# Three quarters of a kernel's opening products from un-normed x, with g_pre folded into the weights

## The chip, the cores and the metric

The kernel runs on one core of a Trainium2 chip. The metric is the device time of one execution in microseconds. TensorE (PE) multiplies, VectorE (DVE) and ScalarE (ACT) work on tiles element by element, GpSimd (POOL) and SyncE (SP) mostly issue transfers here. Every engine takes its own instructions in order.

## The reference

One decoder layer, x of 512 tokens by 2048 channels, float32. What matters here is its first step:

```
h = x * rsqrt(mean(x * x, axis=-1) + 1e-6) * g_pre
[q | k | v | z_att | u | g_glu | z_conv] = h @ w_in
conv = layernorm(causal_conv31(u * sigmoid(g_glu)) + conv_b) ...
```

Attention over q, k, v, the convolution branch, an output projection and a second norm follow; they are computed as before.

## The kernel before

Every float32 factor is split into a rounded high part (hi) and a rest (lo), and a product is three matmuls: hi*hi, hi*lo, lo*hi. The high part is an ACT copy, the rest a DVE subtraction (`split`).

**The opening** computes the first 512 channels of g_glu, token rows by channels, in 16 blocks (kg, m): kg is one of four groups of 512 input channels, m one of four groups of 128 tokens. `turn_x` (`turn_block` in the plan) transposes the x tile of a block on PE in four 128x128 matmuls, ACT writes the high part `h_hi`, DVE the rest `h_lo`. `rows_block` is the block's 12 matmuls into the PSUM tile `gn` of its m; the transposes of the next block stand behind its first two matmuls. `part` splits a 128x512 piece of the weights (`r_gn` into `h_gn`, `l_gn`).

For kg = 0 the kernel already works without the norm: the weights are multiplied by g_pre (`g_col`), x is taken as it is, and each `gn` is later multiplied by its token's root (`scale_up`). For kg = 1 to 3 x is normed first: `square` and `root` give the root of each token, `broadcast_g` spreads g_pre over 128 partitions with two matmuls a group, and `scale_block` multiplies x by both before it is transposed. The normed h of kg = 0, which the later products need, is made by `norm_first` at the end of the opening from a kept copy of the transposed x (`whole`).

**The order.** PE's order is the order of the code. In the opening DVE and ACT too run in code order, given by the table `plan`: what stands behind each block's matmuls. Later DVE, ACT, SP and POOL are ordered by the scheduler.

**Behind the opening** come the first products of the pair u (`pair`): two steps of 48 matmuls, one for each half of the 2048 input channels, with weights `r_u` of 1 MB each. `turn_vectors` transposes the ten rows of conv_w, conv_b, ln_g, ln_b and b_pw2 into `vec` (tile `rows`, two halves of five transfers: 31 rows of 2 KB for conv_w, one row of 2 KB for each of the others). `turn_gates` transposes the finished g_glu (`g_nat`, copied from `gn`) into `gT`. Both stand inside the first step of u.

**Transfers.** SP's queue carries x, weights and `rows`. POOL's queue carries sums of weight blocks (`vs`, 1 MB each, some of them accumulating in DRAM), one issued after each block from the sixth on. A transfer from SP also waits until the one eight places before it has landed (the DMAHW numbers below go round from 0 to 7). Raw weights have two buffers, so a transfer into one waits until DVE has split what was there.

Of the kernel before, what the change touches and what calls it, by code (L numbers as in the profile page):

```python
# [16 lines left out]
P = 128  # L17
# [31 lines left out]
def hybrid_layer(  # L49
# [81 lines left out]
    pick = const.tile([4, 4, P], F32R, name="pick")  # L131
    for j in range(4):
        nc.gpsimd.tensor_copy(pick[:, j, :], ident[:4, j : j + 1].to_broadcast([4, P]))
# [15 lines left out]
    g_ks = early.tile([4, P], F32, name="g_ks")  # L149
    g_col = const.tile([P, 4], F32, name="g_col")  # L150
    g_rows = t2("g_rows")[:4]
    g_bc = {}

    def turn_g():

        ps = trp.tile([P, S], F32, tag="tr", name="g_col_ps")
        nc.tensor.transpose(ps[:, :4], g_ks, ident[:4, :4])
        nc.vector.tensor_copy(g_col, ps[:, :4])

    def split_g():  # L160
        g_parts = [t2(f"g_{part}", F32R)[:4] for part in ("hi", "lo")]
        split(*g_parts, g_rows)
        return g_parts

    def broadcast_g(j, g_hi, g_lo):

        ps = trp.tile([P, S], F32, tag="tr", name=f"g_ps{j}")
        nc.tensor.matmul(ps, pick[:, j, :], g_hi, start=True, stop=False)
        nc.tensor.matmul(ps, pick[:, j, :], g_lo, start=False, stop=True)
        g_bc[j] = t2(f"g_bc{j}")  # L170
        nc.vector.tensor_copy(g_bc[j], ps)
# [28 lines left out]

    def square(m, j, eng=None):
        junk = t2(f"junk{m}_{j}")
        total = sums[m][:, j : j + 1]
        if eng is None:
            nc.scalar.activation(junk, xts[m][j], AF.Square, accum_out=total)
        else:
            eng.tensor_tensor_reduce(
                out=junk, in0=xts[m][j], in1=xts[m][j], scale=1.0, scalar=0.0,
                op0=ALU.mult, op1=ALU.add, accum_out=total,
            )  # L210
# [3 lines left out]
    def root_table(m):  # L214
# [6 lines left out]
        rsqrt_table(y, v)  # L221
        roots[m] = y, v

# [15 lines left out]
    def turn_x(m, j):  # L239
# [9 lines left out]
        if j == 0:  # L249
            nc.scalar.copy(raw_h[m, 0], src)  # L250
        nc.vector.tensor_tensor(out=lo, in0=src, in1=f32(hi), op=ALU.subtract)

        def keep_raw():
            raw_h[m, j] = t2(f"xw{m}_{j}").rearrange("p (i t) -> p i t", i=4)
            nc.scalar.copy(raw_h[m, j], src)
# [21 lines left out]
    def norm_first():  # L277

        lo = {}
        for i in range(5):  # L280
            if i < 4:
                x, hi = whole[:, i, :], h_hi[0][:, i, :]
                nc.vector.scalar_tensor_tensor(
                    out=x, in0=x, scalar=g_col[:, i : i + 1], in1=rbc[0],
                    op0=ALU.mult, op1=ALU.mult,
                )
                nc.scalar.activation(hi, x, AF.Copy)
            if i > 0:
                nc.vector.tensor_tensor(
                    out=h_lo[0][:, i - 1, :], in0=whole[:, i - 1, :], in1=f32(h_hi[0][:, i - 1, :]),  # L290
                    op=ALU.subtract,
                )
            yield
# [39 lines left out]
    def pair(c0, post, name, halves=(0, 1)):  # L333
# [3 lines left out]
        def unit(half, i):  # L337
            def go(w):
                hi, lo = w
                if half == halves[0]:  # L340
                    ps[i] = mm(f"{name}_{i}")
                cs = slice(i * P, (i + 1) * P)
                for k in range(8):
                    mm3(
                        ps[i], (hi[:, k, cs], lo[:, k, cs]), h_at(half * 8 + k),
                        half == halves[0] and k == 0, half == halves[1] and k == 7,
                    )
                if half == halves[1]:
                    post(i, ps[i])
            return go  # L350

        for half in halves:
# [646 lines left out]
    def conv_in(t):  # L999
        if t > 1:  # L1000
            pair(C_G + t * 256, post_g(2 * t), f"g{t}")

        pair(C_U + t * 256, post_u(2 * t), f"u{t}", (0, 1) if t else (1, 0))
# [31 lines left out]
    with tc.manual_schedule(engines={mybir.EngineType.DVE, mybir.EngineType.Activation}):  # L1035
# [5 lines left out]
        def load_w0(kg, eng=nc.sync):  # L1041
            raw, hi, lo = (
                raws.tile([P, 4, S], F32, tag="raw", name=f"r_gn{kg}"),
                his.tile([P, 4, S], F32R, tag="hi", name=f"h_gn{kg}"),
                los.tile([P, 4, S], F32R, tag="lo", name=f"l_gn{kg}"),
            )
            w0[kg] = raw, hi, lo
            if kg == 0:
                for i in range(4):
                    eng.dma_start(raw[:, i], g_src(0)[i * P : (i + 1) * P, :])  # L1050
            else:
                eng.dma_start(raw, g_src(kg).rearrange("(k p) c -> p k c", p=P))

        def part(kg, i):
            raw, hi, lo = w0[kg]
            split(hi[:, i], lo[:, i], raw[:, i], g_col[:, i : i + 1] if kg == 0 else None)
# [11 lines left out]
        nc.sync.dma_start(g_ks, g_pre[: 4 * P].rearrange("(k p) -> k p", p=P))  # L1068
        load_x(0, 0)
        load_w0(0, nc.scalar)  # L1070
        nc.sync.dma_start(g_rows, g_pre.rearrange("(j c) -> j c", j=4))
        for m in range(1, NT):
            load_x(m, 0)
        load_x(0, 1, 2, 3)
        load_x(1, 1, 2, 3)
        load_w0(1)
        load_x(2, 1, 2, 3)
        load_x(3, 1, 2, 3)

        turn_g()  # L1080
        blocks = [(kg, m) for kg in range(4) for m in range(NT)]

# [10 lines left out]
        def do(f, *args):  # L1093
            return partial(f, *args)

        g_parts = []
        first = norm_first()
        keeps = {}

        plan = {  # L1100
            0: ([do(turn_block, 2)], [
                lambda: g_parts.extend(split_g()), do(square, 0, 1), do(square, 0, 2, dve),
                do(square, 0, 3),
            ]),
            1: ([do(turn_block, 3), lambda: broadcast_g(1, *g_parts)], [
                do(root_table, 0), do(square, 1, 1), do(square, 1, 2, dve), do(root, 0),
                do(square, 1, 3), do(root_table, 1), 
            ]),
            2: ([lambda: broadcast_g(2, *g_parts)], [
                do(scale_block, 4), do(part, 1, 0), do(scale_up, 0), do(root, 1),  # L1110
                do(scale_block, 5), do(part, 1, 1),
            ]),
            3: ([do(turn_block, 4), lambda: broadcast_g(3, *g_parts)], [
                do(square, 2, 1), do(part, 1, 2), do(square, 2, 2, dve), do(part, 1, 3),
                do(square, 2, 3), do(root_table, 2), do(scale_up, 1),
            ]),
            4: ([do(turn_block, 5)], [
                do(root, 2), do(scale_block, 6), do(square, 3, 1), do(square, 3, 2, dve),
                do(square, 3, 3), do(root_table, 3), do(scale_up, 2), do(load_w0, 2),
            ]),  # L1120
            5: ([do(turn_block, 6)], [
                do(root, 3), do(scale_block, 7), do(scale_up, 3), do(part, 2, 0), do(part, 2, 1),
            ]),
            6: ([do(turn_block, 7)], [do(scale_block, 8), do(part, 2, 2), do(part, 2, 3)]),
            7: ([do(turn_block, 8)], [do(scale_block, 9), do(scale_block, 10)]),
            8: ([do(turn_block, 9)], [do(load_w0, 3), do(scale_block, 11), do(part, 3, 0)]),
            9: ([do(turn_block, 10)], [do(scale_block, 12), do(part, 3, 1)]
                + [do(widen_root, m) for m in range(NT)]),
            10: ([do(turn_block, 11)], [
                load_vectors,  # L1130
                do(scale_block, 13), do(part, 3, 2), do(part, 3, 3)
            ]),
            11: ([do(turn_block, 12), broadcast_roots], [
                do(scale_block, 14)
            ]),
            12: ([do(turn_block, 13)], [
                do(scale_block, 15), lambda: loaded.update({0: steps[0].load()}),
            ]),
            13: ([do(turn_block, 14)], [do(keep_rows, 0)]),
            14: ([do(turn_block, 15)], [  # L1140
                do(keep_rows, 1), do(next, first)
            ]),
            15: ([], [do(next, first), do(keep_rows, 2), do(next, first)]),
        }
        loaded = {}
# [3 lines left out]
        turn_block(1)  # L1149
        for m in range(NT):  # L1150
            square(m, 0, dve)
        for n, (kg, m) in enumerate(blocks):
            if n < 4:
                for f in plan[n][0]:
                    f()
            rows_block(kg, m, ps0[m], w0[kg][1:], plan[n][0] if n >= 4 else ())
            for f in plan[n][1]:
                f()
            if 4 <= n + 1 < len(blocks):
# [4 lines left out]
        next(first)  # L1164
        next(first)
# [11 lines left out]

    heads_run = attention()
# [8 lines left out]
    for n, step in enumerate(steps):  # L1187
# [23 lines left out]
        if n + 1 < len(steps):  # L1211
# [43 lines left out]
```

## Time and profile before

| | |
|---|---|
| median of 3 runs | 878.05 us (875.48 to 878.66) |
| the profiled execution's own time | 875.07 us |
| its span in the profile | 873.4 us |
| PE busy | 852.9 us, 98% of the span |
| DVE, ACT, POOL busy | 625.2, 392.3, 125.9 us |

Busy is the time in which an engine had at least one instruction in work. The span is the profiled part of an execution; its own time is 1.7 us longer. A busy PE is not necessarily a PE at its full rate, since matmuls overlap: its rate is read from the starts of neighbouring matmuls.

### The profile page before, as it was taken

The page shows a single profiled execution, that of the slowest core. Times are in us where ns is not written, and L with a number is a line of the kernel's source. Part 1 is how long each engine was busy: PE and PEld are TensorE (multiplying, and loading weights), DVE is VectorE, ACT ScalarE, POOL GpSimd, SP SyncE. Part 2 cuts the span into 40 slices and gives each one's busy share as a digit, 9 for nine tenths or more (in the row PEclk, how much of TensorE's full clock was granted, in tenths as well). Part 3 has the DMA queues.
Part 4 walks back from the last instruction along what each step waited for, and adds up shares of the span by engine and source line. Part 5 has one row for each costly group of instructions (what it writes and reads, how often), then busy time and mean ns, then how long its engine had stood idle before and what let it go on. Part 6 is the DMA issues. An engine that isn't in the chain of part 4 may idle for free.

```text
span 873.4 us, 9762 instructions
## 1 busy us (share of the span) xinstructions
PE 852.9 (98%) x3879; PEld 706.5 (81%) x3879; DVE 625.2 (72%) x742; ACT 392.3 (45%) x447; POOL 125.9 (14%) x157
## 2 busy tenths in 40 slices
PE   6899999999999999999999999999999999999995
PEld 4688888888888888888888888888888888888884
DVE  5766889996697978969696984235643776458775
ACT  5653424645443543343322545235722346455542
POOL 0012110001202132213111233032001000000032
PEclk9999999999999999999999999999999999999998
DMA  9499994558587565875497547862232246556782
GB/s 300 160 266 257 282 278 149 193 192 293 192 191 150 176 204 130 174 188 185 144 189 151 190 147 191 167 171 96 90 104 97 97 158 227 193 193 259 283 275 98
DMA packets 87262, 163.32 MB, mean 187 GB/s; under 512 B 2978, under 2 KB 52134, under 8 KB 83440
## 3 DMA queue, kind: packets, MB, share of 16 engines
q1 hardware_dynamic: 70320, 111.31, 37.6%
q0 software_dynamic: 16320, 50.33, 25.4%
q10 hardware_dynamic: 576, 1.05, 0.4%
q8 instruction: 30, 0.49, 0.2%
q14 instruction: 16, 0.13, 0.0%
HBM read 158.49 MB, written 54.53 MB: 244 GB/s over the span
## 4 chain that ended last, share of the span: by engine, by line
PE 87%; DVE 7%; ACT 2%; issue 2%; DMA 1%; DVEq 0%; SPq 0%; ACTq 0%
PE u L326 3%; PE u L328 3%; PE q L328 3%; PE u L327 3%; PE za L328 3%; PE zc L328 3%; PE q L327 3%; PE za L327 3%; PE zc L327 3%; PE za L326 3%; PE a L923 3%; PE q L326 3%; PE a L922 3%; PE zc L326 3%; PE a L924 3%; PE k L326 3%
## 5 line engine op out<-in xcount | busy, mean ns | idle before, releaser
L383 DVE SCALAR_TENSOR_TENSOR acc<-hg,vec,acc 128x512 f32<-128x512 f32 x240 | 182.3, 760 | 6.9
L100 DVE TENSOR_TENSOR l_w<-r_w,h_w 128x2048 fp32r<-128x2048 f32 x28 | 64.1, 2291 | 42.3 <-ACT h_w L99 42.3
L99 ACT ACTIVATE h_w<-r_w 128x2048 fp32r<-128x2048 f32 x28 | 53.5, 1915 | 43.6 <-DMA r_w<-ws 11.4
L326 PE MATMUL u<-h_hi,h_u 128*128 128x512 f32 x128 | 50.2, 392 | 0.0
L326 PE MATMUL q<-h_hi,h_q 128*128 128x512 f32 x128 | 50.1, 391 | 0.0
L326 PE MATMUL k<-h_hi,h_k 128*128 128x512 f32 x128 | 50.0, 391 | 0.0
L326 PE MATMUL za<-h_hi,h_za 128*128 128x512 f32 x128 | 49.9, 390 | 0.0
L328 PE MATMUL u<-h_hi,l_u 128*128 128x512 f32 x128 | 49.9, 390 | 0.0
L326 PE MATMUL zc<-h_hi,h_zc 128*128 128x512 f32 x128 | 49.9, 390 | 0.0
L328 PE MATMUL q<-h_hi,l_q 128*128 128x512 f32 x128 | 49.9, 390 | 0.0
L327 PE MATMUL u<-h_lo,h_u 128*128 128x512 f32 x128 | 49.9, 390 | 0.0
L327 PE MATMUL q<-h_lo,h_q 128*128 128x512 f32 x128 | 49.9, 390 | 0.0
L328 PE MATMUL za<-h_hi,l_za 128*128 128x512 f32 x128 | 49.8, 389 | 0.0
L327 PE MATMUL za<-h_lo,h_za 128*128 128x512 f32 x128 | 49.8, 389 | 0.0
L328 PE MATMUL zc<-h_hi,l_zc 128*128 128x512 f32 x128 | 49.8, 389 | 0.0
L328 PE MATMUL k<-h_hi,l_k 128*128 128x512 f32 x128 | 49.8, 389 | 0.0
L327 PE MATMUL k<-h_lo,h_k 128*128 128x512 f32 x128 | 49.8, 389 | 0.0
L327 PE MATMUL zc<-h_lo,h_zc 128*128 128x512 f32 x128 | 49.8, 389 | 0.0
L922 PE MATMUL a<-h_w,f_hi 128*128 128x512 f32 x128 | 49.8, 389 | 0.0
L923 PE MATMUL a<-l_w,f_hi 128*128 128x512 f32 x128 | 49.8, 389 | 0.0
L924 PE MATMUL a<-h_w,f_lo 128*128 128x512 f32 x128 | 49.8, 389 | 0.0
L653 POOL TENSOR_SCALAR_AFFINE_SELECT t<-t 128x128 f32<-128x128 f32 x64 | 35.7, 636 | 81.9 <-DVE t L676 48.9
(338 smaller groups left out, 2119.7 us busy)
## 6 DMA issues: line engine op xcount, KB each, us to landing
ws<-in_w_out_dram POOLq DMA_DIRECT2D x24, 1024.0 KB, 9.3
r_w<-ws SPq DMA_DIRECT2D x16, 1024.0 KB
vs<-in_w_in_dram POOLq DMA_DIRECT2D x12, 1024.0 KB, 13.8
r_w<-in_w_out_dram SPq DMA_DIRECT2D x12, 1024.0 KB
r_u<-in_w_in_dram SPq DMA_DIRECT2D x8, 1024.0 KB
r_q<-in_w_in_dram SPq DMA_DIRECT2D x8, 1024.0 KB
r_k<-in_w_in_dram SPq DMA_DIRECT2D x8, 1024.0 KB
r_v<-vs SPq DMA_DIRECT2D x8, 1024.0 KB
```

Source lines behind the costliest of these rows:

```text
L99: nc.scalar.activation(hi, src, AF.Copy)
L100: nc.vector.tensor_tensor(out=lo, in0=src, in1=f32(hi), op=ALU.subtract)
L326: nc.tensor.matmul(ps, wh, ah, start=first, stop=False)
L327: nc.tensor.matmul(ps, wh, al, start=False, stop=False)
L328: latest[0] = nc.tensor.matmul(ps, wl, ah, start=False, stop=last).ins
L383: bgq.append(lambda j=j: nc.vector.scalar_tensor_tensor(out=acc, in0=hg[:, j : j + S], scalar=vec[:, ct, j : j + 1], in1=acc, op0=ALU.mult ...
L653: nc.gpsimd.affine_select(out=blk, in_=blk, compare_op=ALU.is_gt, fill=0.0, base=0, pattern=[[-1, P]], channel_multiplier=1,)
L922: nc.tensor.matmul(ps, fh[:, kk, ts], hi[:, k, :], start=st, stop=False, skip_group_check=True)
L923: nc.tensor.matmul(ps, fh[:, kk, ts], lo[:, k, :], start=False, stop=False, skip_group_check=True)
L924: nc.tensor.matmul(ps, fl[:, kk, ts], hi[:, k, :], start=False, stop=en, skip_group_check=True)
```

## The change

For kg = 0, 1 and 2 the blocks are now computed from x as it is, with weights times g_pre (`g_col` has 12 columns for 4); only kg = 3 is normed first. `broadcast_g` with its matmuls is gone, and the one row of g_pre that is still spread over partitions is loaded by a transfer (`load_g`). Squares and roots run beside blocks 1 to 8, `scale_up` comes after kg = 2. `norm_first` now makes h for three groups from the kept transposed x: kg = 1 and 2 by tokens, kg = 0 by channels. The first loads all stand on SP's queue in the order of use, weights of kg = 2 and 3 on POOL's. `turn_vectors` and `turn_gates` stand ahead of u, u takes its halves in the order 0, 1, and within each half channels 512 to 1023 first.

```
     def norm_first():
-        lo = {}
-        for i in range(5):
-            if i < 4:
-                x, hi = whole[:, i, :], h_hi[0][:, i, :]
...
+        def norm(x, i, ts):
+            nc.vector.scalar_tensor_tensor(
+                out=x, in0=x, scalar=g_col[:, i : i + 1], in1=rbc[0][:, ts],
+                op0=ALU.mult, op1=ALU.mult,
+            )
+        def by_tokens(j, m):
+            x, ts = raw_h[m, j], slice(m * P, (m + 1) * P)
+            for i in range(4):
+                norm(x[:, i, :], 4 * j + i, ts)
+            return h_hi[j][:, :, ts], h_lo[j][:, :, ts], x
+        def by_channels(j, i):
...
+        todo = [(f, j, n) for j, f in ((1, by_tokens), (0, by_channels), (2, by_tokens)) for n in range(4)]
...
+            split(hi[:, i], lo[:, i], raw[:, i], g_col[:, k : k + 1] if kg < 3 else None)
...
+        for m in range(NT):
+            load_x(m, 1)
+        load_w0(1)
+        for m in range(NT):
+            load_x(m, 2, 3)
+        load_g(3)
...
-            2: ([lambda: broadcast_g(2, *g_parts)], [
-                do(scale_block, 4), do(part, 1, 0), do(scale_up, 0), do(root, 1),
...
+            7: [
+                do(part, 2, 2), do(root_table, 2), do(root, 1), do(part, 2, 3), do(root_table, 3),
+            ],
...
+            11: [
+                do(part, 3, 3), do(scale_block, 14), do(scale_up, 2), do(next, first),
+                load_vectors,
+            ],
+            12: [do(scale_block, 15), do(next, first), do(scale_up, 3), do(next, first)],
+            13: [lambda: loaded.update({0: steps[0].load()}), do(keep_rows, 0)],
...
+        loaded[1] = steps[1].load()
...
+    turn_vectors()
+    turn_gates()
     heads_run = attention()
...
-            if n == 0 and unit is step.units[-1]:
-                turn_gates()
-            if n == 0 and unit is step.units[0]:
-                turn_vectors()
```

PE at the program's start, before: three x tiles are transposed ahead of the first block's matmuls (`xT` is a transposed tile, `gn` the block's product).

```order
L244 MATMUL xT_0_179<-ident,x_0_105 128x128 [waits DMAHW1_49]
L244 MATMUL xT_0_179<-ident,x_0_105 128x128 x3
L244 MATMUL xT_0_195<-ident,x_0_109 128x128 [waits DMAHW5_49]
L244 MATMUL xT_0_195<-ident,x_0_109 128x128 x3
L244 MATMUL xT_0_211<-ident,x_0_113 128x128 [waits DMAHW7_49]
L244 MATMUL xT_0_211<-ident,x_0_113 128x128 x3
L453 MATMUL gn_141<-h_gn_150,h_hi_121 128x512 [waits Activation_49]
```

The same place now:

```order
L237 MATMUL xT_0_174<-ident,x_0_100 128x128 [waits DMAHW0_49]
L237 MATMUL xT_0_174<-ident,x_0_100 128x128 x3
L463 MATMUL gn_135<-h_gn_144,h_hi_116 128x512 [waits Activation_49]
L464 MATMUL gn_135<-l_gn_145,h_hi_116 128x512 [waits DVE_49]
L237 MATMUL xT_0_192<-ident,x_0_104 128x128 [waits DMAHW4_49]
L237 MATMUL xT_0_192<-ident,x_0_104 128x128 x3
L463 MATMUL gn_135<-h_gn_144,h_hi_116 128x512 [waits Activation_49]
```

The first two matmuls of the block now come behind one transposed tile, and the second tile behind them.

PE at the end of the opening, before: the last matmuls of block 15, the first of u, and 24 matmuls further on the transposes of `rows`, which wait for the ten transfers.

```order
L460 MATMUL gn_144<-h_gn_507,h_lo_128 128x512 x3
L326 MATMUL u_0_732<-h_hi_123,h_u_638 128x512
...
L328 MATMUL u_0_732<-h_hi_124,l_u_639 128x512
L191 MATMUL vec_ps<-ident,rows_566 128x35 [waits DMAHW4_49,DMAHW5_49,DMAHW3_49,DMAHW6_49,DMAHW2_49,Activation_49]
L191 MATMUL vec_ps<-ident,rows_566 128x35 x3
L191 MATMUL vec_ps<-ident,rows_572 128x35 [waits DMAHW3_49,DMAHW2_49,DMAHW7_49,DMAHW1_49,DMAHW0_49]
```

The same place now:

```order
L470 MATMUL gn_138<-h_gn_321,h_lo_123 128x512 x3
L179 MATMUL vec_ps<-ident,rows_564 128x35 [waits DMAHW3_49,DMAHW2_49,DMAHW4_49,DMAHW1_49,DMAHW0_49]
L179 MATMUL vec_ps<-ident,rows_564 128x35 x3
L179 MATMUL vec_ps<-ident,rows_570 128x35 [waits DMAHW6_49,DMAHW2_49,DMAHW7_49,DMAHW1_49,DMAHW0_49]
L179 MATMUL vec_ps<-ident,rows_570 128x35 x3
L1185 MATMUL gT_744<-ident,g_nat_640 128x128 [waits PE_49]
...
L334 MATMUL u_0_772<-h_hi_117,h_u_635 128x512
```

Both sets of transposes moved ahead of all of u, the ones of `rows` directly behind the opening's last block.

SP's queue, before, from the first weights of u on (`rows_566` and `rows_572` are the two halves of the small rows):

```order
L311 DMA r_u_637<-in_w_in_dram 128x8x256 [waits DMAHW7_49,DMAHW1_49,DVE_49]
L184 DMA rows_566<-in_conv_w_dram 31x512 [waits DMAHW2_49]
...
L186 DMA rows_566<-in_b_pw_dram 1x512 [waits DMAHW6_49]
L184 DMA rows_572<-in_conv_w_dram 31x512 [waits PE_49]
...
L186 DMA rows_572<-in_b_pw_dram 1x512 [waits DMAHW3_49]
L311 DMA r_u_726<-in_w_in_dram 128x8x256 [waits DMAHW4_49,DVE_49]
```

The same place now:

```order
L319 DMA r_u_634<-in_w_in_dram 128x8x256 [waits DMAHW7_49,DMASW0_49,DVE_49]
L172 DMA rows_564<-in_conv_w_dram 31x512 [waits DMAHW0_49]
...
L174 DMA rows_564<-in_b_pw_dram 1x512 [waits DMAHW4_49]
L319 DMA r_u_718<-in_w_in_dram 128x8x256 [waits DMAHW5_49,DMASW1_49,DVE_49]
L172 DMA rows_570<-in_conv_w_dram 31x512 [waits DMAHW6_49]
L174 DMA rows_570<-in_conv_b_dram 1x512 [waits DMAHW7_49]
L174 DMA rows_570<-in_ln_g_dram 1x512 [waits DMAHW0_49]
L174 DMA rows_570<-in_ln_b_dram 1x512 [waits DMAHW1_49]
L174 DMA rows_570<-in_b_pw_dram 1x512 [waits DMAHW2_49]
```

The second weights of u now stand between the two halves of `rows`; before they stood behind both.

## Rows read from the trace of the kernel before

**Rows 1.** The page, busy time of an engine, its share of the span and its instructions.

```profile
PE 852.9 (98%) x3879; PEld 706.5 (81%) x3879; DVE 625.2 (72%) x742; ACT 392.3 (45%) x447; POOL 125.9 (14%) x157
```

**Rows 2.** Three stretches: the blocks 1 to 15, the first products behind them, and a stretch at the very end behind PE's last matmul. Columns: stretch, its length, busy time (instructions) of PE, PEld, DVE, ACT, POOL, the granted clock of PE as a share of the full one, DMA share, GB/s.

```profile
16.40:68.60 52.20, 49.91 (x238) 39.25 (x237) 38.41 (x81) 32.43 (x68) 5.06 (x6) 1.00 0.79 234
68.60:93.00 24.40, 24.40 (x121) 20.21 (x120) 15.22 (x21) 10.51 (x14) 5.14 (x5) 1.00 1.01 272
...
866.00:868.00 2.00, 0.00 (x0) 0.00 (x0) 2.00 (x3) 0.26 (x1) 1.66 (x1) 0.50 0.36 133
```

**Rows 3.** Whom PE waited for, over the whole span: us in total, times, the longest.

```profile
PE xT L244 <- DMA x<-in_x_dram: 4.8, 3, 3.4
...
PE xT L244 <- DVE x L231: 2.2, 2, 1.3
PE g_ps L169 <- DVE g_lo L100: 1.0, 1, 1.0
```

**Rows 4.** PE in order of time, the start of the program. Columns: start, length, instruction, in brackets the idle time ahead and who ended it. The row at 13.99 is the first behind block 0, the one at 16.48 the first of block 1.

```profile
6.00 1.11 PE L244 MATMUL xT<-ident,x 128*128 128x128 f32 x4 [3.39 <-DMA x<-in_x_dram]
8.26 1.12 PE L244 MATMUL xT<-ident,x 128*128 128x128 f32 x4 [1.15 <-DMA x<-in_x_dram]
...
11.38 0.63 PE L453 MATMUL gn<-h_gn,h_hi 128*128 128x512 f32 x1
11.80 0.53 PE L454 MATMUL gn<-l_gn,h_hi 128*128 128x512 f32 x1
12.17 0.39 PE L453 MATMUL gn<-h_gn,h_hi 128*128 128x512 f32 x1
12.40 0.39 PE L454 MATMUL gn<-l_gn,h_hi 128*128 128x512 f32 x1
...
13.99 0.60 PE L244 MATMUL xT<-ident,x 128*128 128x128 f32 x4
...
16.48 0.50 PE L453 MATMUL gn<-h_gn,h_hi 128*128 128x512 f32 x1
```

**Rows 5.** PE in order of time: the transposes in two neighbouring blocks, the first row of block 15, the first of u.

```profile
43.48 0.60 PE L244 MATMUL xT<-ident,x 128*128 128x128 f32 x4
...
46.69 0.60 PE L244 MATMUL xT<-ident,x 128*128 128x128 f32 x4
...
65.88 0.39 PE L453 MATMUL gn<-h_gn,h_hi 128*128 128x512 f32 x1
...
68.60 0.39 PE L326 MATMUL u<-h_hi,h_u 128*128 128x512 f32 x1
```

**Rows 6.** PE in order of time: the transposes of `rows` and of `g_nat` with the row behind each.

```profile
74.13 0.68 PE L191 MATMUL vec_ps<-ident,rows 35*128 35x35 f32 x8
74.74 0.50 PE L326 MATMUL u<-h_hi,h_u 128*128 128x512 f32 x1
...
80.33 1.91 PE L1174 MATMUL gT<-ident,g_nat 128*128 128x128 f32 x16
82.00 0.48 PE L326 MATMUL u<-h_hi,h_u 128*128 128x512 f32 x1
```

**Rows 7.** SP's queue in order of time. The first column is when a transfer is issued; x2 stands for two in a row, the time that of the first.

```profile
41.31 0.37 SPq L311 DMA_DIRECT2D r_u<-in_w_in_dram  x1
41.73 0.43 SPq L184 DMA_DIRECT2D rows<-in_conv_w_dram  x1
...
42.56 0.75 SPq L186 DMA_DIRECT2D rows<-in_ln_g_dram  x1
...
48.82 0.22 SPq L186 DMA_DIRECT2D rows<-in_ln_g_dram  x1
54.66 0.22 SPq L186 DMA_DIRECT2D rows<-in_ln_b_dram  x1
...
56.43 0.39 SPq L311 DMA_DIRECT2D r_u<-in_w_in_dram  x1
62.10 16.50 SPq L311 DMA_DIRECT2D r_q<-in_w_in_dram  x2
```

**Rows 8.** Whom SP's queue waited for between 26 and 105 us, with the columns of rows 3.

```profile
SPq L186 <- DMA rows<-in_conv_w_dram: 5.6, 1, 5.6
...
SPq L311 <- DMA rows<-in_ln_g_dram: 1.1, 1, 1.1
```

**Rows 9.** ACT and DVE in order of time: the splits of the weights of u (its first half, then its second) and of the first of q, with the waits for their transfers.

```profile
59.78 2.29 DVE L100 TENSOR_TENSOR l_u<-r_u,h_u 128x2048 fp32r<-128x2048 f32 x1 [0.45 <-ACT h_u L99]
...
73.97 1.92 ACT L99 ACTIVATE h_u<-r_u 128x2048 fp32r<-128x2048 f32 x1 [4.59 <-DMA r_u<-in_w_in_dram]
...
87.52 1.92 ACT L99 ACTIVATE h_q<-r_q 128x2048 fp32r<-128x2048 f32 x1 [9.03 <-DMA r_q<-in_w_in_dram]
89.47 2.29 DVE L100 TENSOR_TENSOR l_q<-r_q,h_q 128x2048 fp32r<-128x2048 f32 x1 [4.88 <-ACT h_q L99]
```

**Rows 10.** Prices of operations between 5 and 69 us, grouped by line and shape: busy us, mean ns of one, idle time ahead of them and who ended it.

```profile
L251 DVE TENSOR_TENSOR h_lo<-xT,h_hi 128x512 fp32r<-128x512 f32 x16 | 11.0, 689 | 16.3 <-ACT h_hi L248 10.8 <-ACT whole L250 5.4
...
L283 DVE SCALAR_TENSOR_TENSOR whole<-whole,g_col,rbc 128x512 f32<-128x512 f32 x4 | 2.9, 745 | 0.0
...
L264 DVE COPY wide<-y 128x128 f32<-128x128 f32 x4 | 0.6, 224 | 0.0
```

**Rows 11.** DVE in order of time: the last splits of the weights of kg = 2.

```profile
40.00 1.29 DVE L100 TENSOR_TENSOR l_gn<-r_gn,h_gn 128x512 fp32r<-128x512 f32 x2
```

More of the change, by code (lines that the diff above doesn't have):

```diff
@@ L156, in turn_g, with load_g @@
         ps = trp.tile([P, S], F32, tag="tr", name="g_col_ps")
[L157 to L169, printed above, removed]
+        nc.tensor.transpose(ps[:, :12], g_ks, ident[:12, :12])
+        nc.vector.tensor_copy(g_col, ps[:, :12])
+    def load_g(j):
         g_bc[j] = t2(f"g_bc{j}")
-        nc.vector.tensor_copy(g_bc[j], ps)
+        nc.sync.dma_start(g_bc[j], g_pre[j * S : (j + 1) * S].partition_broadcast(P))
     NV = TAPS + 4
@@ L277, in norm_first @@
     def norm_first():
-        lo = {}
-        for i in range(5):
-            if i < 4:
-                x, hi = whole[:, i, :], h_hi[0][:, i, :]
[L283 to L286, printed above, removed]
-                nc.scalar.activation(hi, x, AF.Copy)
[L288 to L292, printed above, removed]
+        def norm(x, i, ts):
[9 more added lines that the diff above has]
+        def by_channels(j, i):
+            x = whole[:, i, :]
+            norm(x, i, slice(0, S))
+            return h_hi[j][:, i, :], h_lo[j][:, i, :], x
+        todo = [(f, j, n) for j, f in ((1, by_tokens), (0, by_channels), (2, by_tokens)) for n in range(4)]
+        made = []
+        for n in range(len(todo) + 2):
+            if n < len(todo):
+                f, j, i = todo[n]
+                made.append(f(j, i))
+            if 1 <= n <= len(todo):
+                hi, _, x = made[n - 1]
+                nc.scalar.activation(hi, x, AF.Copy)
+            if n >= 2:
+                hi, lo, x = made[n - 2]
+                nc.vector.tensor_tensor(out=lo, in0=x, in1=f32(hi), op=ALU.subtract)
             yield
@@ L1094, in do @@
             return partial(f, *args)
-        g_parts = []
         first = norm_first()
-        keeps = {}
+        loaded = {}
         plan = {
[L1101 to L1108, printed above, removed]
-            2: ([lambda: broadcast_g(2, *g_parts)], [
-                do(scale_block, 4), do(part, 1, 0), do(scale_up, 0), do(root, 1),
[L1111 to L1129, printed above, removed]
-                load_vectors,
[L1131 to L1143, printed above, removed]
@@ new lines, in hybrid_layer @@
+            5: [
+                do(square, 2, 2), do(square, 2, 3, dve), do(root_table, 0), do(square, 3, 2),
+                do(square, 3, 3, dve), do(root_sum, 1),
+            ],
+            6: [
+                do(part, 2, 0), do(root_table, 1), do(root, 0), do(part, 2, 1), do(root_sum, 2),
+                do(root_sum, 3),
+            ],
+            7: [
+                do(part, 2, 2), do(root_table, 2), do(root, 1), do(part, 2, 3), do(root_table, 3),
+            ],
+            8: [do(part, 3, 0), do(root, 2), do(root, 3)]
+                + [do(widen_root, m) for m in range(NT)],
@@ L1144, in hybrid_layer @@
+            14: [do(keep_rows, 1), do(next, first), do(next, first)],
+            15: [do(keep_rows, 2), do(next, first)],
         }
-        loaded = {}
         turn_block(0)
@@ L1148, in hybrid_layer @@
             part(0, i)
-        turn_block(1)
-        for m in range(NT):
-            square(m, 0, dve)
+        keeps[0]()
         for n, (kg, m) in enumerate(blocks):
[L1153 to L1157, printed above, removed]
+            rows_block(
+                kg, m, ps0[m], w0[kg][1:], [do(turn_block, n + 1)] if n + 1 < len(blocks) else ()
+            )
+            for f in plan[n]:
                 f()
-            if 4 <= n + 1 < len(blocks):
+            if n + 1 < len(blocks):
                 keeps[n + 1]()
@@ L1163, in hybrid_layer @@
         keep_rows(3)
-        next(first)
-        next(first)
+        for _ in range(4):
+            next(first)
+        loaded[1] = steps[1].load()
+        for _ in first:
+            pass
         floor[0] = tc.cur_priority
@@ L1210, in hybrid_layer @@
             sum_next(sumq)
-        if n + 1 < len(steps):
+        if n + 1 < len(steps) and n + 1 not in loaded:
             loaded[n + 1] = steps[n + 1].load()
```

101 lines of the change are left out of this document (59 added, 42 removed).

## The prediction

> **What bounds the kernel now.** I read the busy line first: PE works 98% of the span [rows 1]. Then the stretches: from 68.60 to 93.00 us PE has no gap, while in the opening it is busy for 49.91 of 52.20 us [rows 2]. The waits say where the rest goes: 4.8 us for the first x tiles, 2.2 us for x tiles that DVE still norms, 1.0 us ahead of `broadcast_g` [rows 3]. So time can be won or lost only by what PE does or waits for up to the first products of u, and a microsecond there stays until the end, unless a later transfer eats it. DVE at 72% and ACT at 45% matter only where PE waits for them. I follow one quantity: when PE has finished block 15, `vec_ps` and `gT`. Now block 15 ends at 68.60 [rows 5], and `vec_ps` and `gT`, inside u, take 0.61 and 1.67 us of PE [rows 6]: 68.60 + 0.61 + 1.67 = 70.88.
>
> **The front.** Now three transposed tiles stand ahead of block 0's matmuls; the first starts at 6.00, the matmuls at 11.38, block 1's at 16.48 [rows 4]. In the changed kernel the first x tile is the first transfer of SP's queue and two matmuls need only that tile. When it lands no row shows. It can't be much earlier than PE's first instruction before its 3.39 us wait, which ended at 6.00, so from 2.6 [rows 4], and at the latest about 5.6, with nothing won but an issue or so of 0.4 us (the pitch of issues in [rows 7]). I take 4.0, in the middle. Behind it: 1.1 us of transposes [rows 4], the high part and h_lo (some 0.7 each), two matmuls, the second tile, then ten matmuls at the slow pitch of 0.42 us (11.38 to 11.80), or at 0.23 once the clock is up (12.17 to 12.40) [rows 4]. With four splits of 0.69 us for the first weights on DVE [rows 10] between, block 0 ends near 12.2 (10.7 to 13.5 for the bounds). Gain 16.48 - 12.2 = **4.3 us** (3 to 5.8).
>
> **Blocks 1 to 15.** Now 16.48 to 68.60 is 52.12 us. The pitch of a block where nothing waits is 46.69 - 43.48 = 3.21 us, the last has no transposes behind it: 68.60 - 65.88 = 2.72 [rows 5]. After: 14 x 3.21 + 2.72, and the four transposes of the roots, a quarter of `gT`'s sixteen, 0.42: 48.1 us. Gone are the eight matmuls of `broadcast_g` and the waits of 2.2 and 1.0 us. Gain **4.0 us**; block 15 ends at 12.2 + 48.1 = 60.3.
>
> This holds if DVE and ACT keep pace with 3.21 us a block. Twelve of sixteen x tiles need no norm ahead of PE, so h_lo follows h_hi at once. The new norms by tokens are four 128x128 operations each; the nearest rows are a copy of that size, 224 ns, and the 128x512 norm, 745 ns [rows 10]: between 0.19 (a quarter) and 0.75 each. I take 0.22, the same number of elements, so 0.9 a tile and 1.6 with its h_lo, half a block's time. Eight such tiles, four of them behind block 15, are hidden by 48 matmuls of u's first half (11 us at 0.23). At 0.75 the first four tiles cost 16 x (0.75 - 0.22) = 8.5 us more beside blocks 10 to 13, where DVE is idle for some 4 x 0.92 us ((52.20 - 38.41) / 15 a block [rows 2]); u's first h_lo would then be late by up to 4.8 us. Squares and roots stand beside blocks 1 to 8, where DVE no longer scales. Cost 0, up to 4.8.
>
> **The wait that takes their place.** `vec_ps` needs all ten transfers of `rows`. It now stands directly behind block 15, at 60.3, where it stood at 74.13 and waited for nothing [rows 6]. So the landing R of the last of them decides. SP's queue before: the first `r_u` issued at 41.31, as soon as DVE had split `r_gn` of kg = 2 (40.00 + 1.29 [rows 11]), then `rows`. Ln_b of the second half waited until the first conv_w had landed, 54.66, so 12.9 us for 62 KB, while the `r_u` of 1 MB ahead of it was there by about 48.82, 7.5 us; the second `r_u` waited for the first ln_g until 56.43, and landed at 73.97, 17.5 us; the first `r_q` took from 62.10 to 87.52, 25.4 us [rows 7 to 9].
>
> The same conditions set the times after. The splits for kg = 2 end in block 7, which starts at 12.2 + 6 x 3.21 = 31.5, about 4.2 us into it: 35.7 for the first `r_u` and, behind it, the first half of `rows`. The last split for kg = 3 is in block 11 (starts 44.3): the second `r_u` near 47.8, and only behind it the second half of `rows`. POOL's sums move too: one is issued per block from the sixth on, now from about 28.3.
>
> How long for the four (`r_u`, `rows`, `r_u`, `rows`)? Before, the same four members took 73.97 - 41.31 = 32.66 us, in another order. Shifted: **R = 35.7 + 32.66 = 68.4**. Low bound: the second `r_u` in 7.5 us and a conv_w behind it in 7.6 (48.82 to 56.43) and 0.8 for the small ones, 63.7. High: with 17.5 for `r_u`, 73.7; with `r_q`'s 25.4, 81.6. I take 68.4, since sums run beside the four at about the same distance as before.
>
> The Trainium skill (DMA: Bandwidth & Descriptors, "Why a DMA increments its semaphore by 16 and not by 1") says that a transfer issued by SP is dealt to the largest number of engines, at most 16, that divides its outermost size: for 31 rows, or for one, a single engine. The trace agrees in its outcome, 12.9 us for 62 KB beside 7.5 for 1 MB. By that rule the ten stay slow wherever they are queued, and the sum keeps its wait; if they were spread as `r_u` is, the rival "rows in time" below would be the likeliest.
>
> **Price of the wait.** PE idles from 60.3 to 68.4, 8.1 us. Behind its last matmul the profile shows a granted clock of 0.50, the level of 1.2 GHz, against 1.00 (2.4 GHz) in the busy stretches [rows 2]; at the start PE works slowly from 8.26 until the pitch falls to 0.23 at 12.17, 3.9 us [rows 4]. I charge the same at the restart: 3.9 us at half speed lose 1.95, so `vec_ps` and `gT` take 2.28 + 1.95 = 4.23 us. Bounds: nothing, and 1.95. With R = 68.4 PE is through at 72.6, against 70.88 before: **+1.75 us**. In general the difference is R - 66.65. Queued behind `vec_ps` are `gT` and u, so all of PE; DVE stands at its copy `vec`, ahead of the second split of u, which is not due for 11 us more.
>
> **Sum.** -4.3 - 4.0 + 8.1 + 1.95 = +1.75 on the profiled 875.07 (span 873.4 and 1.7 around it): 876.8. The median of the runs lies 2.98 above the profiled one: **879.8 us**.
>
> **Rivals.**
> *A longer wait (the other side).* The second `r_u` takes 17.5 us as it did, now ahead of the second `rows`: R = 73.7, +7.05, so 875.07 + 7.05 + 2.98 = 885.1; with 25.4 us 893.0. It makes the kernel slower from R = 71.0 on. For it: sums and `r_u` run together from 47.8. Against: in before that `r_u` itself stood behind the slow rows.
> *Rows in time.* R at or below 60.3: 60.3 + 2.28 = 62.6 against 70.88, -8.3, 869.8. For it: the first `rows` get 24 us before they are needed. Against: the second are issued only 12.5 us ahead, and conv_w alone took 12.9. Then `r_q` is next: its buffer is free when u's first half is split, at 62.07 before (59.78 + 2.29 [rows 9]), now behind block 14's h_hi near 59.8. With its 25.4 us and the same splits (87.52 to 91.76 [rows 9]) its low part is there at 89.4, where PE wants it at 93.0 - 8.3 + 0.5 = 85.2: 4.2 us given back, 873.9. So 869.8 to 873.9.
> *DVE late.* Norms at 0.75 us each: with `rows` at 68.4 the 4.8 us lie inside that wait and the time stays 879.8; with rows in time it is 869.8 + 4.8 = 874.6, no change.
>
> **Chances.** A measurement of this kernel tells about 0.5%, 4.4 us, from no change: faster below 873.7, slower above 882.4. Forecast, R between 62.3 and 71.0: 0.40, 874 to 882. Rows in time: 0.30, of which 0.25 are faster and 0.05 same, since `r_q` may give half back. A longer wait: 0.30, slower. So 0.25, 0.45, 0.30. The range leaves out the best 0.1 and the worst 0.1: 869 (rows in time, nearly whole) to 887 (R = 75.6).
>
> **What would show it.** The first transposes near 4.0 and block 1 at 12.2; blocks at a pitch of 3.21 without waits for DVE x; block 15's end at 60.3; issues of `r_u` near 35.7 and 47.8; `vec_ps` with an idle time of 8 us put down to a transfer of `rows`, a granted clock of 0.50 ahead of it, and u from 72.6. Wrong would be a `vec_ps` without a wait (then the look goes to q's first matmuls and `r_q`), a wait beyond 71, or block pitches above 3.21 with waits for h_lo.

## The result and the profile after

The changed kernel takes 880.85 us (median of 20 runs, 879.41 to 883.64), the kernel before in the 20 runs beside it 879.04: a ratio of 1.0038 (95% interval 1.0023 to 1.0053). That is inside the 0.5% that I had called no change, on the slow side: the interval leaves out a ratio of 1 and ends just above 0.5%. The profiled execution took 880.67 us with a span of 878.9.

The page of the changed kernel, busy time of each engine (for [rows 1]):

```profile
PE 852.7 (97%) x3873; PEld 708.8 (81%) x3873; DVE 630.9 (72%) x770; ACT 396.7 (45%) x454; POOL 126.4 (14%) x155
```

PE's work is the same to 0.2 us. What differs is where it waits. Whom PE waited for, over the whole span (for [rows 3]):

```profile
PE vec_ps L179 <- DMA rows<-in_b_pw_dram: 10.3, 1, 10.3
PE g_col_ps L153 <- DMA g_ks<-in_g_pre_dram: 4.1, 1, 4.1
PE gn L463 <- ACT h_gn L102: 1.3, 1, 1.3
PE xT L237 <- DMA x<-in_x_dram: 0.5, 1, 0.5
```

The waits for normed x and ahead of `broadcast_g` are gone, and a wait of 10.3 us for the last row of `rows` has come. PE in order of time, the front and the end of the opening (for [rows 4, 5, 6]):

```profile
4.87 1.12 PE L237 MATMUL xT<-ident,x 128*128 128x128 f32 x4 [0.52 <-DMA x<-in_x_dram]
7.28 0.79 PE L463 MATMUL gn<-h_gn,h_hi 128*128 128x512 f32 x1 [1.29 <-ACT h_gn L102]
...
13.41 0.40 PE L463 MATMUL gn<-h_gn,h_hi 128*128 128x512 f32 x1
...
58.86 0.39 PE L463 MATMUL gn<-h_gn,h_hi 128*128 128x512 f32 x1
...
61.67 0.43 PE L179 MATMUL vec_ps<-ident,rows 35*128 35x35 f32 x4
72.45 0.61 PE L179 MATMUL vec_ps<-ident,rows 35*128 35x35 f32 x4 [10.34 <-DMA rows<-in_b_pw_dram]
73.00 3.67 PE L1185 MATMUL gT<-ident,g_nat 128*128 128x128 f32 x16
76.32 0.78 PE L334 MATMUL u<-h_hi,h_u 128*128 128x512 f32 x1
...
77.75 0.43 PE L334 MATMUL u<-h_hi,h_u 128*128 128x512 f32 x1
```

Block 1 starts at 13.41 and the opening ends at 61.67, 6.9 us earlier than the 68.60 before. Then the first four transposes of `rows` run; the last four wait until 72.45. The stretches around that wait, with columns as in [rows 2]:

```profile
13.30:61.60 48.30, 48.30 (x242) 39.56 (x240) 37.94 (x92) 36.76 (x78) 6.87 (x8) 1.00 0.93 283
61.60:72.40 10.80, 0.51 (x5) 0.32 (x4) 5.93 (x15) 3.30 (x5) 2.72 (x3) 0.62 1.11 232
72.40:77.70 5.30, 5.25 (x23) 4.97 (x24) 2.41 (x7) 3.55 (x7) 0.00 (x0) 0.50 1.06 333
77.70:98.90 21.20, 21.20 (x94) 17.49 (x93) 16.76 (x26) 7.08 (x9) 3.40 (x4) 1.00 0.93 242
```

Blocks 1 to 15 have no gap. The granted clock falls within the wait (0.62 on average there) and stands at 0.50, 1.2 GHz, in the 5.3 us of work behind it, against 1.00 before and after. SP's queue (for [rows 7]):

```profile
36.99 0.38 SPq L319 DMA_DIRECT2D r_u<-in_w_in_dram  x1
37.41 0.48 SPq L172 DMA_DIRECT2D rows<-in_conv_w_dram  x1
...
49.40 0.40 SPq L319 DMA_DIRECT2D r_u<-in_w_in_dram  x1
49.84 0.43 SPq L172 DMA_DIRECT2D rows<-in_conv_w_dram  x1
...
58.22 0.22 SPq L174 DMA_DIRECT2D rows<-in_b_pw_dram  x1
59.20 23.17 SPq L319 DMA_DIRECT2D r_q<-in_w_in_dram  x2
```

The second `r_u`, with the time from issue to landing at the end of the row:

```profile
r_u<-in_w_in_dram SPq DMA_DIRECT2D x1, 1024.0 KB, 14.0
```

So the second `r_u` lands at 49.4 + 14.0 = 63.4, and the rows behind it 9 us later.

### The profile page after: what moved, and what is told of

Same layout as the page of the kernel before. It is cut to its first block, busy times and chain, and to the rows that moved or that the text cites. A ratio compares the mean times of both kernels' runs of the same rounds, so it can differ in the third digit from the quotient of the medians.

```text
span 878.9 us, 9789 instructions
## 1 busy us (share of the span) xinstructions
PE 852.7 (97%) x3873; PEld 708.8 (81%) x3873; DVE 630.9 (72%) x770; ACT 396.7 (45%) x454; POOL 126.4 (14%) x155
## 4 chain that ended last, share of the span: by engine, by line
PE 94%; DMA 4%; DVE 1%; ACT 0%; issue 0%; SPq 0%; DVEq 0%
PE u L335 3%; PE u L334 3%; PE u L336 3%; PE k L334 3%; PE za L334 3%; PE q L335 3%; PE q L334 3%; PE zc L334 3%; PE k L335 3%; PE a L932 3%; PE za L336 3%; PE zc L335 3%; PE q L336 3%; PE za L335 3%; PE zc L336 3%; PE k L336 3%
```

## The experiments

Theory A is that the wait comes from a transfer whose rows run one behind another; the expectations name the theories that it is tested against. Each kernel ran beside the kernel before, and ratios are against that. They depend on how many of those runs came from the upper of two groups of times (below), so the versions are compared by their times.

**conv_w in two pieces, in the changed kernel.**

```
-            nc.sync.dma_start(rows[half][0:TAPS], conv_w.rearrange("k o c -> (k o) c")[:, cs])
+            taps = conv_w.rearrange("k o c -> (k o) c")
+            nc.sync.dma_start(rows[half][0:16], taps[0:16, cs])
+            nc.sync.dma_start(rows[half][16:TAPS], taps[16:TAPS, cs])
```

> The changed kernel, but the 31 rows of conv_w go as two transfers, of 16 and of 15 rows, for each half of `rows`; nothing else is edited. Theory A (the wait of `vec_ps` comes from transfers of many rows that run as one row behind another): the two pieces land a microsecond or two behind the second `r_u` ahead of them, so R falls from 72.45 to between 60 and 65, the idle time ahead of `vec_ps` from 10.3 us to 0 to 3.5 us, the slow clock at u's start is gone or short, and the kernel takes 7 to 12 us less than the changed one (profiled 869 to 874). Theory B (the second half of `rows` is late because it stands behind 1 MB of `r_u` and beside the sums, however it is cut): R stays at 68 or more, the time within 3 us of the changed kernel. Theory C (DMA as a whole limits the stretch from 60 to 100 us): the wait goes, but u's second half or q waits for weights, and less than half of the 12 us comes back.

870.32 us, ratio 0.9922 (0.9896 to 0.9948). PE at the end of the opening:

```profile
61.50 0.69 PE L181 MATMUL vec_ps<-ident,rows 35*128 35x35 f32 x8
62.12 0.55 PE L1187 MATMUL gT<-ident,g_nat 128*128 128x128 f32 x3
62.93 1.64 PE L1187 MATMUL gT<-ident,g_nat 128*128 128x128 f32 x13 [0.26 <-ACT g_nat L1079]
64.32 0.48 PE L336 MATMUL u<-h_hi,h_u 128*128 128x512 f32 x1
```

The second `r_u` and the first piece of the second half behind it, issued at 49.22 and 50.13:

```profile
r_u<-in_w_in_dram SPq DMA_DIRECT2D x1, 1024.0 KB, 11.9
rows<-in_conv_w_dram SPq DMA_DIRECT2D x1, 32.0 KB, 11.2
```

All eight transposes run without a wait, and u starts 12 us earlier than in the changed kernel (76.32). The second `r_u` is issued as before and lands at 61.1 in place of 63.4, the sums are issued up to 2.3 us earlier, and the piece behind `r_u` lands at 61.3, 0.2 us later in place of 9. So theory B falls: cutting the rows is enough. 10.5 us come back. Theory C falls too, since q waits for no weights.

**The transposes late, the transfers as they are.** `turn_gates` and `turn_vectors` go back into u.

```
-    turn_vectors()
-    turn_gates()
...
+            if n == 0 and unit is step.units[-1]:
+                turn_gates()
+            if n == 1 and unit is step.units[0]:
+                turn_vectors()
```

> The changed kernel, but `turn_gates` stands behind u's first step (as before the change) and `turn_vectors` behind the first unit of u's second step, some 18 us into u; transfers are issued as in the changed kernel. Theory A: `vec_ps` then stands at about 79 us, R is 72.5 as before, no wait; u starts at about 62 instead of 76.3. DVE makes the last h_lo of kg = 1 at 62.3 and of kg = 0 until about 67, so u's first unit waits 1 to 3 us for DVE; the kernel takes 9 to 13 us less than the changed one. Theory C: q waits for `r_q` by several us, and less than half comes back.

876.16 us, ratio 0.998 (0.9956 to 1.0004): only 4.7 us less than the changed kernel. PE in order of time, and ACT's split of the first `r_q`:

```profile
81.80 0.68 PE L179 MATMUL vec_ps<-ident,rows 35*128 35x35 f32 x8
...
88.44 0.50 PE L334 MATMUL q<-h_hi,h_q 128*128 128x512 f32 x1 [0.28 <-ACT h_q L99]
...
90.77 0.50 PE L336 MATMUL q<-h_hi,l_q 128*128 128x512 f32 x1 [1.59 <-DVE l_q L100]
```

```profile
86.47 1.92 ACT L99 ACTIVATE h_q<-r_q 128x2048 fp32r<-128x2048 f32 x1 [11.86 <-DMA r_q<-in_w_in_dram]
```

`vec_ps` waits for nothing, as expected, but the wait has moved to q: its weights are landed only at 86.5. That was theory C's outcome, and its cause is the next question.

**Late transposes and conv_w in pieces together** (the two edits above).

> The late transposes of e2_late and the 16 and 15 rows of e1_spread together. e2_late had no wait of `vec_ps` and yet gave most of its gain back: `r_q` was landed only at 86.5 us (78 to 80 in e1_spread and e3_early) and q waited 3.5 us. Theory A2 (the rows that run one behind another hold up the share of `r_q` behind them too): with the rows in pieces `r_q` lands near 80, q starts without a wait, and the time is that of e1_spread, 868 to 871. Theory D (late transposes let PE reach q too early, so that it waits for `r_q` whatever else is done): q waits 2 us or more, the time stays 873 to 876.

869.68 us, ratio 0.9925 (0.9897 to 0.9954). The same split:

```profile
77.36 1.92 ACT L99 ACTIVATE h_q<-r_q 128x2048 fp32r<-128x2048 f32 x1 [3.80 <-DMA r_q<-in_w_in_dram]
```

9 us earlier than in e2_late, with nothing else changed but the cut of conv_w: the rows had held up the weights behind them too. q waits for nothing, and theory D falls.

**`rows` loaded earlier.** `load_vectors` moves from block 11 to block 6 of the plan, ahead of both `r_u`.

```
             6: [
-                do(part, 2, 0), do(root_table, 1), ...
+                load_vectors, do(part, 2, 0), do(root_table, 1), ...
...
             11: [
...
-                load_vectors,
```

> The changed kernel, but `rows` are loaded at block 6 of the plan, so that they stand on SP's queue directly behind the first loads and ahead of both `r_u`; `turn_vectors` stays directly behind block 15. Theories A and B: all ten land before 50 us, `vec_ps` waits for nothing, u starts at about 64 instead of 76.3, with a wait of at most 1 us for h_lo; 10 to 13 us less than the changed kernel. Theory C: the wait goes and q or u's second half waits for weights, less than 6 us come back.

870.39 us, ratio 0.9912 (0.988 to 0.9943). `vec_ps` runs without a wait:

```profile
62.03 0.69 PE L179 MATMUL vec_ps<-ident,rows 35*128 35x35 f32 x8
```

Early and in pieces are worth the same.

**The old order on SP's queue.** `load_vectors` moves only to block 9: first `r_u`, all of `rows`, second `r_u`, conv_w in one piece.

```
             9: [
-                do(part, 3, 1), broadcast_roots, do(scale_block, 12), do(scale_up, 0),
+                load_vectors, do(part, 3, 1), broadcast_roots, do(scale_block, 12), do(scale_up, 0),
...
             11: [
...
-                load_vectors,
```

> The changed kernel with `rows` loaded two blocks earlier in the plan, so that SP's queue has the order of the kernel before again: the first `r_u`, both halves of `rows`, the second `r_u`; conv_w in one piece, `vec_ps` directly behind block 15. f3_before_ahead showed that with this order the last of `rows` was there by 68.70, 27 us behind the issue of the first conv_w (41.74). Theory A3 (the order on the queue makes R late, the rows' own slowness is the other half): issued at about 37.5, they land by 64.5 at the latest, the wait of `vec_ps` is 0 to 3 us instead of 10.3 and the time 870 to 876. Theory A4 (one piece of 31 rows is late wherever it stands): the wait stays at 6 us or more, 877 or more.

876.19 us, ratio 1.0005 (0.999 to 1.0019), just above the 870 to 876 of theory A3. PE in order of time, and ACT's split of the second `r_u`:

```profile
63.99 0.41 PE L179 MATMUL vec_ps<-ident,rows 35*128 35x35 f32 x4 [2.50 <-DMA rows<-in_b_pw_dram]
...
79.33 0.52 PE L334 MATMUL u<-h_hi,h_u 128*128 128x512 f32 x1 [2.13 <-ACT h_u L99]
...
81.65 0.79 PE L336 MATMUL u<-h_hi,l_u 128*128 128x512 f32 x1 [1.38 <-DVE l_u L100]
```

```profile
77.36 1.91 ACT L99 ACTIVATE h_u<-r_u 128x2048 fp32r<-128x2048 f32 x1 [8.73 <-DMA r_u<-in_w_in_dram]
```

The wait of `vec_ps` shrinks from 10.3 to 2.5 us, so the order is a part of R, as theory A3 says. But now the second `r_u` stands behind the slow rows, and u's second half waits for it, 2.1 and 1.4 us. It is split 13 us after the last row was there, so it pays for more than the rows' own time. The order only decides who pays.

**`turn_vectors` ahead of u, in the kernel before.**

```
+    turn_vectors()
     heads_run = attention()
...
-            if n == 0 and unit is step.units[0]:
-                turn_vectors()
```

> The kernel before, with one part of the change alone: `turn_vectors` directly behind block 15, at 68.6 us, instead of 24 matmuls into u. Theory A: the wait depends only on when the last of `rows` lands. In the lower group of the kernel before it is there by 74.1, so `vec_ps` waits for 0 to 5.5 us, and in the upper group longer; with the slow clock behind it the kernel takes 2 to 8 us more than before (median 879 to 885). Theory B' (moving `turn_vectors` alone is harmless, the wait comes from the earlier end of the blocks): within 2 us of the kernel before.

875.08 us, ratio 0.9996 (0.9969 to 1.0023): no change, against theory A's 2 to 8 us. PE and ACT in the profiled execution, which took 878.75 us:

```profile
68.70 0.68 PE L191 MATMUL vec_ps<-ident,rows 35*128 35x35 f32 x8
...
116.02 0.50 PE L326 MATMUL k<-h_hi,h_k 128*128 128x512 f32 x1 [1.07 <-ACT h_k L99]
...
118.34 0.50 PE L328 MATMUL k<-h_hi,l_k 128*128 128x512 f32 x1 [1.59 <-DVE l_k L100]
```

In the order of before the last row is there by 68.70. So moving `turn_vectors` alone is harmless, as theory B' says; in the changed kernel it costs because the blocks end 6.9 us earlier and R comes at least 3.7 us later. The waits for k belong to the next question.

**Where the two groups of times come from.** Times of the kernel before lie near 875 or between 878 and 883. I first took the upper ones for late rows. Three runs bear on it: the kernel before with the edit of conv_w in two pieces, and twice the kernel before as it is.

> The kernel before, but conv_w goes as 16 and 15 rows for each half. There `vec_ps` waits for nothing, so by theory A the time stays within 0.5% of the kernel before, while the second `r_u`, which stood behind the rows, lands several us earlier than 73.97 (between 62 and 70). By theory B that landing does not move. If the time falls by more than 0.5%, transfers of `rows` cost the kernel before something that its profile does not show on PE.

874.76 us; all ten runs lie between 874.63 and 875.12, where of the 26 runs of the kernel before beside them 13 lay above 878. The second `r_u` is split at 69.57 instead of 73.97, between 62 and 70 as theory A expects.

> The kernel before, unchanged, profiled once more. Its runs lie in two groups, near 875 and from 878 to 881, and with conv_w in two pieces (e4_before_spread) only the lower group is left, 874.6 to 875.1. Theory A: the upper group are executions in which the last of `rows` lands behind 74.1 us, so that `vec_ps` waits 1 to 4 us inside u. If this profile is from the upper group (about two in three), PE shows that wait and the span is 876 us or more; if it is from the lower, there is no wait and the span is 873. An upper one without a wait of `vec_ps` would say that the groups have another cause.

874.8 us, from the lower group, without a wait of `vec_ps`: it decides nothing.

> The kernel before, profiled a third time. Two profiles fell into the lower of its two groups (873.1 and 873.4 us), and f3_before_ahead, which has the same two groups, was profiled in its upper one: `vec_ps` waited for nothing, but the first `r_k` was split at 114.05 instead of 104.09 and PE waited 2.7 us for it. Theory F: an upper profile of the kernel before shows the same wait for k and none of `vec_ps`. Another lower profile leaves that open for the kernel before.

878.39 us, from the upper group. `vec_ps` runs without a wait, so my first theory on the groups falls. PE and ACT of this execution:

```profile
74.21 0.68 PE L191 MATMUL vec_ps<-ident,rows 35*128 35x35 f32 x8
...
115.71 0.50 PE L326 MATMUL k<-h_hi,h_k 128*128 128x512 f32 x1 [0.70 <-ACT h_k L99]
...
118.04 0.50 PE L328 MATMUL k<-h_hi,l_k 128*128 128x512 f32 x1 [1.60 <-DVE l_k L100]
```

```profile
113.74 1.91 ACT L99 ACTIVATE h_k<-r_k 128x2048 fp32r<-128x2048 f32 x1 [17.59 <-DMA r_k<-in_w_in_dram]
```

ACT in the kernel before, the execution shown ahead of the prediction:

```profile
104.09 1.92 ACT L99 ACTIVATE h_k<-r_k 128x2048 fp32r<-128x2048 f32 x1 [6.34 <-PE q L328]
```

In both profiles of the upper group (this one and f3_before_ahead) the first `r_k` lands some 10 us later, and PE waits for k; in both of the lower it doesn't. With conv_w in pieces no run of ten is in the upper group. Why it happens in only some of the others is open.

**What takes back the rest.** In e3_early q starts at 86.70, 6.3 us ahead of before, but only 4.7 us are left at the end. The 1.6 us are lost between 130 and 165 us, in the products that follow k (`va`). To see whether DVE takes them, 15 tap additions are left out for each of the first two channel tiles:

```
-            for j in range(1, TAPS):
+            for j in range(1, TAPS if ct >= 2 else 16):
```

> e3_early with 15 of the 30 tap additions left out for the first two channel tiles of the convolution (30 DVE operations of 0.76 us, 22.8 us, beside the work from 94 to 210 us; so the convolution is only partly computed). In e3_early q starts 6.3 us earlier than before, but from 142 us on only 4.7 us are left, with DVE busy for nearly all of 120 to 140 us and PE waiting for `l_v`. Theory E (DVE takes these back): without the additions the waits for `l_v` and `l_k` go and the end keeps 6 to 7 us, 866 to 868 us, 1.5 to 2.5 less than e3_early. Theory C (the weights' transfers take them back): the same waits stay, the time is that of e3_early within 0.7 us.

867.85 us, 2.5 less than e3_early. DVE and PE of e3_early in order of time, and the stretch from 120 to 140 us of e3_early and then of this kernel (columns as in [rows 2]):

```profile
128.55 6.27 DVE L393 SCALAR_TENSOR_TENSOR acc<-hg,vec,acc 128x512 f32<-128x512 f32 x8
134.73 2.28 DVE L100 TENSOR_TENSOR l_v<-r_v,h_v 128x2048 fp32r<-128x2048 f32 x1
```

```profile
137.07 0.50 PE L627 MATMUL va<-l_v,h_hi 128*128 128x512 f32 x1 [1.02 <-DVE l_v L100]
```

```profile
120.00:140.00 20.00, 18.98 (x84) 15.39 (x83) 19.50 (x25) 6.93 (x6) 0.12 (x1) 1.00 0.41 127
```

```profile
120.00:140.00 20.00, 20.00 (x90) 16.57 (x89) 12.79 (x12) 6.50 (x6) 3.12 (x2) 1.00 0.44 151
```

Eight additions stand ahead of `l_v` on DVE, PE waits 1.0 us for it, and DMA is at 0.41: theory E. Without the additions the wait is gone, and nothing is lost between 130 and 165 us: DVE, not the transfers, takes these 1.6 us. Not all of the 2.5 us is theirs: in the profiled execution `vec_ps` already runs at 61.03, 1.0 us earlier than in e3_early, ahead of all additions. The kernel before was not run with fewer additions.

**A version to beat the others.** `turn_gates` ahead of u, `turn_vectors` late, conv_w in pieces; against f2_late_spread:

```
+    turn_gates()
     heads_run = attention()
...
-            if n == 0 and unit is step.units[-1]:
-                turn_gates()
```

> f2_late_spread with `turn_gates` ahead of u again, as in the change, so that its 1.67 us of PE cover the last h_lo of kg = 1, for which u waited 1.1 us in f2_late_spread; `turn_vectors` stays late and conv_w in pieces. Theory: no wait for h_lo of more than 0.5 us, no wait of `vec_ps`, none for `l_v`; the end keeps 7 us against the kernel before in its lower group (span 866 to 867 against 873.4; 867.5 to 869.5 us), and against its runs as a whole the ratio is 0.988 to 0.993. Rival: the weights of q and k set the pace from 75 us on, then q waits and the time is that of f2_late_spread.

870.89 us, ratio 0.9944 (0.9923 to 0.9965): not better. u no longer waits for h_lo, but the 1.6 us wait for `l_v` is there again, as in e1_spread. The versions e1_spread, e3_early, f2_late_spread and this one lie within 1.2 us of each other, and their intervals overlap. All are faster than the kernel before beside them, and some 10 us below the changed kernel's 880.85, whose runs were not beside theirs.

**Three tiles ahead of block 0, in that version.**

```
-        turn_block(0)
+        for n in range(3):
+            turn_block(n)
...
-                kg, m, ps0[m], w0[kg][1:], [do(turn_block, n + 1)] if n + 1 < len(blocks) else ()
+                kg, m, ps0[m], w0[kg][1:], [do(turn_block, n + 1)] if 2 < n + 1 < len(blocks) else ()
```

> g1_best with one part of the change undone: three x tiles are transposed ahead of block 0's matmuls again (loads stay in the new order). Theory of the front (what counts is how many transfers block 0 waits for): the third tile lands near 8 us, block 1 starts at 15 to 16.5 instead of 13.4, and what is lost there, 1.5 to 3 us, stays to the end: 869.5 to 872. Rival (weights and the slow clock set the front, not the tiles): block 1 within 0.7 us of 13.4, the time within 0.7 us of g1_best.

874.09 us, 3.2 more. Of this kernel, then of g1_best, the first matmuls of block 0 and of block 1:

```profile
11.50 0.79 PE L465 MATMUL gn<-h_gn,h_hi 128*128 128x512 f32 x1 [1.29 <-ACT h_gn L102]
...
16.93 0.39 PE L465 MATMUL gn<-h_gn,h_hi 128*128 128x512 f32 x1
```

```profile
7.28 0.79 PE L465 MATMUL gn<-h_gn,h_hi 128*128 128x512 f32 x1 [1.30 <-ACT h_gn L102]
...
12.64 0.40 PE L465 MATMUL gn<-h_gn,h_hi 128*128 128x512 f32 x1
```

Block 1 starts 4.3 us later when block 0 waits for three tiles, a little more than I had expected, and the time is 3.2 us longer. A part of the 4.3 may be chance: with one tile block 1 starts between 12.64 and 13.74 in the profiles of this section.

## Why the prediction was right, and where it was not

The forecast was no change, 879.8 us, by a gain of 8.3 us in the opening that a wait of `vec_ps` eats. The measured median is 880.85, and the mechanism is the one forecast: the wait, its releaser and the slow clock behind it are in the profile, and with the wait taken away in two ways 10.5 us come back. The nearness of the number, though, is luck: two errors of some 3 to 4 us cancel. The medians differ by 1.8 us, as forecast (1.75), but the profiled executions by 5.6.

*The front*: forecast 4.3 us, 3.1 measured (16.48 to 13.41). The first x tile came at 4.87, not 4.0, block 0 then waited 1.3 us for its first weights, and the slow pitch of 0.42 us held past 12.07; in f2_late_spread and g1_best, with the same front, block 1 started at 12.7.

*Blocks 1 to 15*: forecast 48.1 us, 61.67 - 13.41 = 48.26 measured. The pitch of 3.21 us held, DVE and ACT kept pace, and the norms by tokens took 0.28 us each (1.14 for four), near the 0.22 taken.

*The landing R*: forecast 68.4, measured 72.45. This step failed. I shifted the 32.66 us of four transfers before as if their order did not matter. But the end of those 32.66 was the second `r_u`; f3_before_ahead shows that `rows` were there by 68.70 then, at least 5.3 us ahead of it. In the changed kernel the order is reversed. The way that I had kept as the high bound was the right one: second `r_u`, then the rows behind it, 49.4 + 14.0 + 9.0 against 47.8 + 17.5 + 8.4. The issues came 1.3 and 1.6 us later than forecast, most of it from the front. The rows seem to count twice in this: of the sixteen end packets (4 bytes each) that the second `r_u` leaves in the packed trace, fifteen come by 58.6 and the last only at 63.0, with the first half of `rows` ahead of it; in e3_early, with no rows close ahead, the last comes at 59.65.

*The clock*: charged 1.95 us, measured 2.65, above the bound of 1.95: 5.30 us of work at half speed, in place of 3.9.

*The sum*: -3.1 - 3.9 + 10.3 + 2.65 = +6.0 us against +1.75. q's first matmul starts 5.9 us later than before (98.90 and 93.01), the span is 5.5 longer.

*The way to the median*: I added 2.98 us because the median of three runs lay that far above the profiled one. It isn't an offset of every kernel: the profiled execution of before came from the lower of its two groups, and the waits for k that make the upper one are not in the changed kernel, whose profile (880.67) is its median (880.85). Without this the forecast would have been 876.8, 4.0 too low.

*The rivals*: the longer wait, by its own number 885.1, had R within 1.3 us (73.7) and was the better one; with 72.45 its formula gives 875.07 + 5.8 = 880.9, what the profile shows. Rows in time is what e1_spread and e3_early build: 870.3 and 870.4 lie in its 869.8 to 873.9. That is luck too, since the range holds the 2.98 us; without them it is 866.8 to 870.9. The step that I expected to give half of that gain back, `r_q`, was not it: it landed in time when the rows did not hold it up. In e3_early 1.7 us are missing because block 15 ends at 62.03, not 60.3, and 1.6 go to DVE, with the wait of 1.0 us at `l_v` (1.6 in e1_spread).

*The page's rule*: the Trainium skill (DMA: Bandwidth & Descriptors, "Why a DMA increments its semaphore by 16 and not by 1") sends 31 rows to a single engine and 16 rows to 16. What the prediction has it say of one row the page does not state; that a row goes as one packet of 2 KB is what the trace shows. By this rule the kernel could be mended: cut in 16 and 15, the transfer no longer delays itself or the weights behind it. The prediction also drew from it that the sum keeps its wait wherever the ten are queued. That failed: sent well ahead (e3_early) they cost no wait, with conv_w in one piece. Packets of the queue of SP's transfers over the span (number, MB, share), in the changed kernel and in e1_spread:

```profile
q1 hardware_dynamic: 69968, 110.51, 37.0%
q1 hardware_dynamic: 70028, 110.51, 37.2%
```

The bytes are the same, with 60 packets more. In the packed trace all 60 are end packets of 4 bytes, 31 in place of one for each half of `rows`. That fits 16 and 15 engines in place of one, though the trace does not name the engines.

One rival is left open: that the sums make the rows slow. In one piece the rows start singly, 8 in the 2 us from 47.3 us in the changed kernel, beside 202 packets of POOL's queue, but 24 in the 2 us from 56.55 us in h_order9, beside 4. So the sums seem to have a part in it. No run moves the sums, and how much is theirs is not shown.

## What to carry to other kernels

Before work is moved ahead of a long stretch, look at the last transfer that it needs, at what stands ahead of that on the queue in the new order, and take the time from those two, not from a shifted total. A small transfer such as these 31 rows can take longer than a megabyte queued beside it and delay what is queued behind it; cutting it into 16 and 15 rows, or sending it well ahead, was worth 10 us here. A profile is one execution: before its distance to the median is carried over to another kernel, find out which wait makes it.

## What was not expected of the hardware

The kernel before has two groups of times some 4 us apart, and in the profiles of the two one weight transfer, issued within a microsecond of the same time, lands by 104.4 us or only at 113.7 and later. And two transfers of 62 KB, each in one piece, together delayed 1 MB behind them by 9 us (`r_q`, 86.5 against 77.4).
